# The up-projection of a diffusion block: weight sums and the gate product move from GpSimd to VectorE

## The chip, the cores and the metric

One core of a Trainium2 chip runs the whole block as one program. Five engines work beside each other, each through its own queue in order: TensorE (PE, with its weight loads as PEld) multiplies matrices, VectorE (DVE), ScalarE (ACT) and GpSimd (POOL) work element by element, and SyncE (SP) issues most of the DMAs. The metric is the device time of one execution in microseconds (us), lower is better.

## The reference, cut to what matters

The block is a norm, a token mixer (a state-space group and a differential attention group), an output projection, and a gated channel mixer. The change touches the channel mixer alone, and there the first matrix product:

```python
D_MODEL = 1024; SEQ = 1024; D_FF = 2816
def conv_ffn(h, w_up, cw, cb, w_down):
    val, gate = jnp.split(h @ w_up, 2, axis=-1)      # w_up: 1024 x 5632, float32
    gate = dwconv_centred(gate, cw, cb)              # width 3 over the 1024 tokens
    return (jax.nn.silu(gate) * val) @ w_down
```

Everything is float32. The kernel splits each float32 operand into a rounded high part and the low rest, and forms a product as high times high plus low times high plus high times low: three matmuls for one.

## The kernel before, in words

The hidden features lie on the 128 partitions, in 22 blocks of 128 for the value branch (0 to 21) and 22 for the gate branch (`NJ` = 22 onward). The tokens lie along the free dimension in two halves of 512. A `Unit` computes two neighbouring blocks of one branch over both halves with seven block products in place of eight (a Strassen-Winograd scheme). Its two weight tiles A0 and A1 (128 x 1024, 512 KB each, loaded by `raw_w`, four buffers named `wraw`) are each split into two halves of the contraction, so that a unit has four weight blocks, and combines them into sums `S` (`Unit.sums`, line 1205): S1 = A10 + A11, S2 = S1 - A00, S4 = A01 - S2 and S3 = A00 - A10. The matching sums of the activations (T1 to T4, B22) are made once, ahead of the loop.

The seven products of a unit come in the order P1, P2 (`p1`, `p2`, weights taken as they are), P3 (weight S4), P5 (S1), P6 (S2) in `p356`, and T3 (S3) and T4 (A11) in `rest`. Each is 12 matmuls of 128x128 by 128x512 into one of eight PSUM banks named `pu` (4 blocks of the contraction, three matmuls each). TensorE's order is pinned to the order of the code; the other engines' orders are chosen by a scheduler from its own estimate of times, so a change in one engine's load moves rows on others too.

Before a product can start, ScalarE rounds its weights (`whi`, line 125) and GpSimd or VectorE subtracts to get the low part (`wlo`, line 126). `whi` and `wlo` have three buffers each, so the rounding for a product waits until the product three places earlier is done. In the steady loop the low parts of P5 and T4 are VectorE's and the other five GpSimd's.

After the products, `rest` combines them: U2, U4, U3 (`add`, line 1226) and four outputs through `put`. For a gate unit `put_gate` adds into the tile `gt` (line 1251); `conv` then makes `u` by a scaled copy on ScalarE (line 1264), two multiply-adds on VectorE (lines 1265 and 1267) and a SiLU on ScalarE (line 1269). For a value unit `put_val` adds into a scratch tile `v` on VectorE (line 1257), and GpSimd multiplies `v` into `u` (line 1259). `gated` (line 1350) then makes four differences of the gated blocks on VectorE into a tile `T` and sends blocks and differences to memory (`gf_d`), from where the down-projection (`down`, tile names `pd`, `stg`) reads them back. `gt` and `T` share one buffer: the first `gt` of a pair waits until the `T` of the pair before has left.

The loop at the end of the function runs over j = 0, 2, ..., 20, one gate unit and one value unit each. For j = 0 (units `first`) and j = 2 (units `early`) some products are made ahead of the loop, while the activations' sums are still being formed.

Of the kernel before, what the change touches and what calls it, by code (L numbers as in the profile page):

```python
# [8 lines left out]
F32 = mybir.dt.float32  # L9
F32R = mybir.dt.float32r  # L10
AF = mybir.ActivationFunctionType
ALU = mybir.AluOpType
# [4 lines left out]
P = 128  # L17
# [86 lines left out]
class Prog:  # L104
# [934 lines left out]
    def mixffn(self, es, ssd_rest, e_pm):  # L1039
        nc, io = self.nc, self.io  # L1040
# [4 lines left out]
        op = self.pool(e_o, "mo", 2)  # L1045
# [50 lines left out]
        for dt in range(KT):  # L1096
            wa = self.load_w(io["wO"][dt][:, 8:12, :], kt=4)
            nc.sync.dma_start(x1[:, dt, :], io["xT"][:, dt, :])
            for t in range(2):
# [3 lines left out]
                                               in1=x1[:, dt, sls[t]], op0=ALU.mult, op1=ALU.add)  # L1103
# [86 lines left out]
        class Unit:  # L1190
# [11 lines left out]

            def sums(u, in0, in1, op):
                t = wp.tile([P, 4, P], F32, name="S", bufs=S_BUFS)
                nc.gpsimd.tensor_tensor(out=t, in0=in0, in1=in1, op=op)  # L1205
                return t

            def mul(u, src, T, eng=None):
# [30 lines left out]

            def rest(u, put):  # L1240
                U2 = u.add("U2", u.P6, u.X)
                put(0, 0, u.P2, u.X)
                U4 = u.add("U4", u.P5, U2)
                U3 = u.add("U3", u.mul(u.sums(u.sub(0, 0), u.sub(1, 0), ALU.subtract), T3), U2)
                put(0, 1, u.P3, U4)
                put(1, 1, u.P5, U3)
                put(1, 0, u.mul(u.sub(1, 1), T4, nc.vector), U3)

        def put_gate(gt):
            def put(i, t, ps, sb):  # L1250
                nc.vector.tensor_tensor(out=gt[:, i, sls[t]], in0=ps, in1=sb, op=ALU.add)
            return put

        def put_val(us):
            def put(i, t, ps, sb):
                v = vp.tile([P, 512], F32, name="v")
                nc.vector.tensor_tensor(out=v, in0=ps, in1=sb, op=ALU.add)
                o = us[i][:, sls[t]]
                nc.gpsimd.tensor_tensor(out=o, in0=o, in1=v, op=ALU.mult)
            return put  # L1260

        def conv(j, gate):
# [10 lines left out]
        first = Unit(NJ, 1), Unit(0, 1)  # L1273
# [47 lines left out]
        vp = self.pool(e_ffn, "vp", 2, side="right")  # L1321
        for j in range(0, NJ, 2):
# [5 lines left out]
            for u in (gate, val):  # L1328
                put = put_gate(gt) if u is gate else put_val(us)
# [305 lines left out]
```

## Time and profile before

| what | us |
|---|---|
| median of 3 runs | 1826.5 (1822.24 to 1832.29) |
| the profiled execution | 1826.04 |
| its span in the trace | 1824.2 |
| up-projection, starts of its first and last matmul | 1039.6 and 1535.2 |
| of this the pairs j = 4 to 20, nine alike | 1151.6 to 1535.4 |

The page of the profile gives for each engine its busy time and share of the span: TensorE 88%, VectorE 67%, GpSimd 59%, ScalarE 41%. Such shares are means over stages with different limits, so the stage itself is to be read. A busy TensorE is not TensorE at its peak, since a matmul's row also covers its pipeline; what counts is how far apart the matmuls start. The granted clock of TensorE is given as a share of full speed: 1.00 is 2.4 GHz, 0.50 is 1.2 GHz, and a stretch between the two had both.

### The profile page before, as it was taken

The numbers are of one execution on the slowest core, as the hardware profiler recorded it, in microseconds if no ns is written. First come the engines' busy times: TensorE is split into PE (matmuls) and PEld (weight loads), VectorE is DVE, ScalarE is ACT, GpSimd is POOL, SyncE is SP. The second block draws the span as 40 slices with busy tenths as digits, with TensorE's granted clock in tenths as the row PEclk, the third lists the DMA queues.
The fourth block names the chain that finished last, engine by engine and source line by source line (L and its number), as shares of the span: only waits on it lengthen the run. The fifth ranks groups of instructions, "written<-read, shape, count | busy, mean of one in ns | idle before, by whom it ended". The sixth has DMA issues, their size and how long they took to land.

```text
span 1824.2 us, 21276 instructions
## 1 busy us (share of the span) xinstructions
PE 1601.6 (88%) x7588; PEld 1266.8 (69%) x7588; DVE 1222.1 (67%) x1442; ACT 753.6 (41%) x1395; POOL 1081.2 (59%) x710
## 2 busy tenths in 40 slices
PE   6998998996999888888998958989989998989976
PEld 2797877784778655665677746767777776767755
DVE  4569633352656577877764588766667677898886
ACT  4533676631444333444443443333323334344242
POOL 3322678772100155658566767777778887778741
PEclk8999999998999899999999989999999998999997
DMA  8276767667131667447553312222222225744222
GB/s 310 96 241 218 239 217 246 242 215 224 56 104 46 197 218 213 127 143 234 179 166 114 107 47 98 87 87 93 98 87 87 100 99 187 252 156 127 67 75 93
DMA packets 138826, 273.35 MB, mean 150 GB/s; under 512 B 11984, under 2 KB 60544, under 8 KB 138208
## 3 DMA queue, kind: packets, MB, share of 16 engines
q1 hardware_dynamic: 138128, 271.03, 45.0%
q8 instruction: 60, 0.98, 0.2%
q0 software_dynamic: 592, 0.96, 0.2%
q14 instruction: 46, 0.38, 0.1%
HBM read 197.63 MB, written 74.32 MB: 149 GB/s over the span
## 4 chain that ended last, share of the span: by engine, by line
PE 39%; DVE 18%; POOL 17%; DMA 11%; issue 8%; ACT 6%; SPq 0%; POOLq 0%; DVEq 0%; ACTq 0%
PE pu L145 9%; POOL wlo L126 6%; PE pd L145 6%; POOL S L1205 4%; PE lat L145 4%; PE pz L145 3%; PE pb L145 3%; PE sc L145 3%; DMA K<-kd 3%; PE pw L145 2%; DVE T L126 2%; DMA wt<-wmB 2%; DMA gd<-R 2%; PE po L145 2%; DMA R<-atd 2%
## 5 line engine op out<-in xcount | busy, mean ns | idle before, releaser
L145 PE MATMUL pu<-T,whi 128*128 128x512 f32 x1232 | 387.8, 396 | 8.7 <-ACT whi L125 8.7
L145 PE MATMUL pu<-T,wlo 128*128 128x512 f32 x616 | 248.7, 404 | 44.5 <-POOL wlo L126 36.9
L145 PEld LDWEIGHTS pu<-T,whi 128*128 128x128 f32 x1232 | 235.8, 191 | 58.2 <-ACT whi L125 9.1
L126 POOL TENSOR_TENSOR wlo<-wraw,whi 128x512 fp32r<-128x512 f32 (+2 forms) x118 | 163.4, 1388 | 101.3 <-ACT whi L125 101.2
L145 PE MATMUL lat<-hl,w_hi 128*128 128x512 f32 x640 | 204.6, 396 | 3.0 <-DVE tm L685 2.1
L145 PE MATMUL pd<-T,whi 128*128 128x512 f32 x560 | 183.2, 408 | 15.1 <-ACT whi L125 7.5
L126 POOL TENSOR_TENSOR w_lo<-w_raw,w_hi 128x1024 fp32r<-128x1024 f32 (+1 forms) x36 | 82.7, 2299 | 178.7 <-ACT w_hi L125 156.9
L126 POOL TENSOR_TENSOR wlo<-S,whi 128x512 fp32r<-128x512 f32 (+2 forms) x122 | 171.0, 1411 | 27.6 <-ACT whi L125 27.6
L145 PEld LDWEIGHTS pu<-T,wlo 128*128 128x128 f32 x616 | 117.8, 191 | 86.2 <-POOL wlo L126 49.3
L814 DVE TENSOR_REDUCE stat<-sc 128x1 f32<-128x1280 f32 x64 | 95.2, 1488 | 104.2 <-PE sc L145 104.2
L125 ACT CAST whi<-wraw 128x512 fp32r<-128x512 f32 (+2 forms) x140 | 81.3, 583 | 196.8 <-PE pu L145 108.8
L125 ACT CAST whi<-S 128x512 fp32r<-128x512 f32 (+2 forms) x144 | 81.9, 573 | 150.0 <-PE pu L145 94.7
L145 PEld LDWEIGHTS lat<-hl,w_hi 128*128 128x128 f32 x640 | 121.8, 191 | 28.5 <-DVE tm L685 2.5
L145 PEld LDWEIGHTS pd<-T,whi 128*128 128x128 f32 x560 | 109.5, 197 | 44.2 <-DVE T L126 12.3
L815 ACT ACTIVATE et<-sc,stat 128x1280 f32<-128x1280 f32 x64 | 85.1, 1330 | 130.0 <-DVE stat L814 128.4
L145 PE MATMUL sc<-K,S 128*128 128x512 f32 (+1 forms) x384 | 97.5, 390 | 45.8 <-DMA K<-kd 24.1
L145 PE MATMUL pd<-T,wlo 128*128 128x512 f32 x280 | 115.3, 412 | 15.5 <-POOL wlo L126 15.3
L145 PE MATMUL lat<-hl,w_lo 128*128 128x512 f32 x320 | 126.8, 396 | 0.0
L145 PEld LDWEIGHTS sc<-K,S 128*128 128x128 f32 x384 | 73.5, 200 | 72.8 <-ACT et L815 30.1
L538 POOL TENSOR_TENSOR R<-R,never 128x1024 f32<-128x1024 f32 x32 | 80.6, 2533 | 43.1 <-DMA R<-atd 41.4
L542 ACT ACTIVATE R<-R,lna 128x128 f32<-128x128 f32 x256 | 78.3, 393 | 56.7 <-POOL R L538 56.6
L908 POOL TENSOR_TENSOR xw<-xt,dte 128x1024 f32<-128x1024 f32 x18 | 36.8, 2049 | 93.7 <-DMA xt<-xtok 71.4
(280 smaller groups left out, 3682.0 us busy)
## 6 DMA issues: line engine op xcount, KB each, us to landing
wraw<-wUp SPq DMA_DIRECT2D x46, 512.0 KB, 3.3
wt<-wmB SPq DMA_DIRECT2D x32, 512.0 KB, 4.5
R<-atd SPq DMA_DIRECT2D x32, 512.0 KB, 5.6
stg<-gf_d SPq DMA_DIRECT2D x21, 768.0 KB, 4.8
w_raw<-wU SPq DMA_DIRECT2D x28, 512.0 KB, 5.1
gf_d<-T SPq DMA_DIRECT2D x11, 1024.0 KB, 4.2
K<-kd SPq DMA_DIRECT2D x32, 320.0 KB, 7.8
xt<-xtok SPq DMA_DIRECT2D x19, 512.0 KB, 5.2
```

The costliest lines, as they stand in the source:

```text
L125: nc.scalar.copy(hi, src)
L126: (lo_eng or nc.vector).tensor_tensor(out=lo, in0=src, in1=hi, op=ALU.subtract)
L145: self.pe(self.nc.tensor.matmul(out, lhsT=lhsT, rhs=rhs, start=start, stop=stop))
L538: nc.gpsimd.tensor_tensor(out=R[:, d], in0=R[:, d], in1=self.never[:, d].unsqueeze(1).broadcast_to([P, 8, P]), op=ALU.add)
L542: nc.scalar.activation(e, e, AF.Exp, bias=self.lna[:, d, i, h:h + 1], scale=1.0)
L814: nc.vector.tensor_reduce(out=st[:, c:c + 1], in_=sc, axis=AX.X, op=ALU.max, negate=True)
L815: nc.scalar.activation(et, sc, AF.Exp, bias=st[:, c:c + 1], accum_out=acc)
L908: nc.gpsimd.tensor_tensor(out=h3(xw), in0=h3(xt), in1=bc_h(self.dte, d, i), op=ALU.mult)
L1205: nc.gpsimd.tensor_tensor(out=t, in0=in0, in1=in1, op=op)
```

## The change

Three edits in the up-projection:

- the sums S of all units but the two of j = 0 are made on VectorE (80 of 88);
- the value branch is added in place, into the PSUM bank that holds the product, and VectorE multiplies it into `u` from there; the scratch tile `v` goes, except for one output of the early value unit, which is kept in SBUF from before the loop and goes the old way (43 of 44 products move);
- with that, GpSimd keeps the low parts of the weights and little else.

```diff
             def sums(u, in0, in1, op):
                 t = wp.tile([P, 4, P], F32, name="S", bufs=S_BUFS)
-                nc.gpsimd.tensor_tensor(out=t, in0=in0, in1=in1, op=op)
+                (nc.gpsimd if u in first else nc.vector).tensor_tensor(out=t, in0=in0, in1=in1, op=op)
                 return t
...
-                put(0, 0, u.P2, u.X)
+                put(0, 0, u.P2, u.X, u.early)
...
-            def put(i, t, ps, sb):
+            def put(i, t, ps, sb, sbuf=False):
                 nc.vector.tensor_tensor(out=gt[:, i, sls[t]], in0=ps, in1=sb, op=ALU.add)
...
-            def put(i, t, ps, sb):
-                v = vp.tile([P, 512], F32, name="v")
+            def put(i, t, ps, sb, sbuf=False):
+                v = vp.tile([P, 512], F32, name="v") if sbuf else ps
                 nc.vector.tensor_tensor(out=v, in0=ps, in1=sb, op=ALU.add)
                 o = us[i][:, sls[t]]
-                nc.gpsimd.tensor_tensor(out=o, in0=o, in1=v, op=ALU.mult)
+                (nc.vector if v is ps else nc.gpsimd).tensor_tensor(out=o, in0=v, in1=o, op=ALU.mult)
```

The scheduler then orders the queues anew. GpSimd's queue before, over a value unit of the loop: the first rows are sums of the gate unit still to come, mixed with the low parts of the running unit.

```order
L1205 TENSOR_TENSOR S_10186<-wraw_10143 128x512 [waits DMAHW3_49]
L1205 TENSOR_TENSOR S_10188<-S_10186,wraw_10141 128x512 [waits DMAHW7_49,Pool_49]
L126 TENSOR_TENSOR wlo_10006<-wraw_9831,whi_10005 128x512 [waits Activation_49]
L126 TENSOR_TENSOR wlo_10029<-S_10025,whi_10028 128x512 [waits DVE_49,Activation_49]
L1205 TENSOR_TENSOR S_10190<-wraw_10141,S_10188 128x512 [waits Pool_49]
L1205 TENSOR_TENSOR S_10248<-wraw_10141,wraw_10143 128x512 [waits DVE_49]
L1259 TENSOR_TENSOR u_9975<-u_9975,v_10080 128x512 [waits DMAHW5_49,DVE_49]
L126 TENSOR_TENSOR wlo_10063<-S_10023,whi_10062 128x512 [waits Activation_49]
L126 TENSOR_TENSOR wlo_10089<-S_10085,whi_10088 128x512 [waits Activation_49]
L126 TENSOR_TENSOR wlo_10152<-wraw_10141,whi_10151 128x512 [waits Activation_49]
```

After, the same place holds the low parts alone.

```order
L126 TENSOR_TENSOR wlo_9991<-wraw_9816,whi_9990 128x512 [waits Activation_49]
L126 TENSOR_TENSOR wlo_10014<-S_10010,whi_10013 128x512 [waits DVE_49,Activation_49]
L126 TENSOR_TENSOR wlo_10048<-S_10008,whi_10047 128x512 [waits Activation_49]
L126 TENSOR_TENSOR wlo_10073<-S_10069,whi_10072 128x512 [waits Activation_49]
L126 TENSOR_TENSOR wlo_10133<-wraw_10122,whi_10132 128x512 [waits DMAHW7_49,Activation_49]
L126 TENSOR_TENSOR wlo_10152<-wraw_10122,whi_10151 128x512 [waits Activation_49]
```

The sums and the multiplication are gone from between them: what is in front of a low part on GpSimd is now only another low part.

VectorE's queue before, at the end of a value unit and the start of the next gate unit: the last output, the differences T, the low part of P5 and the first `gt`, which waits for the DMA of T and so holds what follows it.

```order
L1257 TENSOR_TENSOR v_10129<-pu_10112,U3_10104 128x512 [waits PE_49]
L1350 TENSOR_TENSOR T_10132<-u_9980,T_10132 128x512 [waits DVE_49,Pool_49]
L1350 TENSOR_TENSOR T_10132<-u_9980,u_9975 128x512
L126 TENSOR_TENSOR wlo_10211<-S_10186,whi_10210 128x512 [waits PE_49,Activation_49]
L1350 TENSOR_TENSOR T_10132<-u_9980,T_10132 128x512 [waits DVE_49,Pool_49]
L1251 TENSOR_TENSOR gt_10149<-pu_10169,X_10167 128x512 [waits DMAHW2_49,DVE_49,PE_49]
L126 TENSOR_TENSOR wlo_10273<-wraw_10143,whi_10272 128x512 [waits DMAHW3_49,Activation_49]
```

After, at the same place.

```order
L1257 TENSOR_TENSOR pu_10094<-pu_10094,U3_10088 128x512 [waits PE_49]
L1259 TENSOR_TENSOR u_9965<-pu_10029,u_9965 128x512 [waits DVE_49]
L1259 TENSOR_TENSOR u_9965<-pu_10094,u_9965 128x512 [waits DVE_49]
L1350 TENSOR_TENSOR T_10113<-u_9965,T_10113 128x512 [waits DVE_49]
L1350 TENSOR_TENSOR T_10113<-u_9965,u_9960 128x512
L1205 TENSOR_TENSOR S_10320<-wraw_10126,S_10318 128x512 [waits Pool_49]
L1350 TENSOR_TENSOR T_10113<-u_9965,T_10113 128x512 [waits DVE_49]
L126 TENSOR_TENSOR wlo_10192<-S_10167,whi_10191 128x512 [waits PE_49,Activation_49]
L1205 TENSOR_TENSOR S_10379<-wraw_10126,wraw_10128 128x512 [waits DVE_49]
L1251 TENSOR_TENSOR gt_10130<-pu_10150,X_10148 128x512 [waits DMAHW2_49,PE_49]
L126 TENSOR_TENSOR wlo_10254<-wraw_10124,whi_10253 128x512 [waits Activation_49]
```

The multiplications stand between the last output and the differences, and two sums (S4 and S3 of the next value unit) around the low part of P5; the order of T, low part and `gt` is as it was.

VectorE's queue before, from the second `gt` of a gate unit to the low part of P5 of the value unit behind it.

```order
L1251 TENSOR_TENSOR gt_10149<-pu_10192,U4_10246 128x512 [waits DVE_49]
L1226 TENSOR_TENSOR U3_10267<-pu_10250,U2_10243 128x512 [waits PE_49]
L1251 TENSOR_TENSOR gt_10149<-pu_10209,U3_10267 128x512 [waits DVE_49]
L1265 SCALAR_TENSOR_TENSOR u_10289<-gt_10149,c_fcw_89,u_10289 128x1023 [waits DMAHW5_49,Activation_49]
L1251 TENSOR_TENSOR gt_10149<-pu_10271,U3_10267 128x512 [waits PE_49]
L1267 SCALAR_TENSOR_TENSOR u_10289<-gt_10149,c_fcw_89,u_10289 128x1023 [waits DVE_49]
L1265 SCALAR_TENSOR_TENSOR u_10294<-gt_10149,c_fcw_89,u_10294 128x1023 [waits DMAHW1_49,DMAHW0_49,Activation_49]
L1267 SCALAR_TENSOR_TENSOR u_10294<-gt_10149,c_fcw_89,u_10294 128x1023 [waits DVE_49]
L126 TENSOR_TENSOR wlo_10360<-S_10335,whi_10359 128x512 [waits PE_49,Activation_49]
```

After, at the same place, with the sum that now stands ahead of it.

```order
L1205 TENSOR_TENSOR S_10477<-wraw_10434 128x512 [waits DMAHW3_49,Pool_49]
L1251 TENSOR_TENSOR gt_10130<-pu_10173,U4_10227 128x512 [waits DVE_49]
L1205 TENSOR_TENSOR S_10479<-S_10477,wraw_10432 128x512 [waits DMAHW7_49,DVE_49,Pool_49]
L1226 TENSOR_TENSOR U3_10248<-pu_10231,U2_10224 128x512 [waits PE_49]
L1251 TENSOR_TENSOR gt_10130<-pu_10190,U3_10248 128x512 [waits DVE_49]
L1265 SCALAR_TENSOR_TENSOR u_10270<-gt_10130,c_fcw_89,u_10270 128x1023 [waits DMAHW5_49,Activation_49]
L1251 TENSOR_TENSOR gt_10130<-pu_10252,U3_10248 128x512 [waits PE_49]
L1267 SCALAR_TENSOR_TENSOR u_10270<-gt_10130,c_fcw_89,u_10270 128x1023 [waits DVE_49]
L1205 TENSOR_TENSOR S_10481<-wraw_10432,S_10479 128x512 [waits Pool_49]
L1265 SCALAR_TENSOR_TENSOR u_10275<-gt_10130,c_fcw_89,u_10275 128x1023 [waits DMAHW1_49,DMAHW0_49,Activation_49]
L1267 SCALAR_TENSOR_TENSOR u_10275<-gt_10130,c_fcw_89,u_10275 128x1023 [waits DVE_49]
L126 TENSOR_TENSOR wlo_10341<-S_10316,whi_10340 128x512 [waits PE_49,Activation_49]
```

Three sums have come in ahead of that low part. The first of them waits for a weight load (`DMAHW3`).

## Rows read from the trace of the kernel before

**Rows 1.** Chain that ended last: shares of the span by engine and by line

```profile
PE 39%; DVE 18%; POOL 17%; DMA 11%; issue 8%; ACT 6%; SPq 0%; POOLq 0%; DVEq 0%; ACTq 0%
PE pu L145 9%; POOL wlo L126 6%; PE pd L145 6%; POOL S L1205 4%; PE lat L145 4%; PE pz L145 3%; PE pb L145 3%; PE sc L145 3%; DMA K<-kd 3%; PE pw L145 2%; DVE T L126 2%; DMA wt<-wmB 2%; DMA gd<-R 2%; PE po L145 2%; DMA R<-atd 2%
```

**Rows 2.** By stretch: length, busy PE, PEld, DVE, ACT, POOL (instructions), granted clock, DMA, GB/s

```profile
1114.20:1151.56 37.36, 29.25 (x121) 21.98 (x120) 32.02 (x28) 13.03 (x18) 29.08 (x17) 1.00 0.28 98
1151.56:1535.43 383.87, 359.32 (x1513) 286.08 (x1511) 255.56 (x235) 127.42 (x184) 300.41 (x201) 0.98 0.29 100
1535.43:1565.00 29.57, 21.95 (x71) 14.43 (x71) 29.52 (x32) 15.11 (x30) 18.47 (x15) 0.83 0.80 282
```

**Rows 3.** The same view: three products without a wait, one product with

```profile
1256.65:1264.81 8.16, 8.16 (x37) 6.76 (x36) 7.72 (x9) 4.20 (x5) 5.41 (x4) 1.00 0.20 64
1219.48:1228.57 9.09, 4.60 (x14) 3.32 (x12) 7.55 (x4) 4.24 (x5) 8.93 (x6) 0.81 0.17 58
```

**Rows 4.** Waits over the nine pairs: us in total, times, longest us

```profile
DVE gt L1251 <- DMA gf_d<-T: 41.7, 9, 5.6
...
PE pu L145 <- POOL wlo L126: 21.3, 15, 4.5
...
POOL S L1205 <- DMA wraw<-wUp: 19.3, 14, 4.0
...
PE pu L145 <- DVE wlo L126: 3.2, 8, 0.6
```

**Rows 5.** Timeline of TensorE in the long wait: start us, us, instruction [idle before]

```profile
1224.35 0.50 PE L145 MATMUL pu<-T,wlo 128*128 128x512 f32 x1 [4.49 <-POOL wlo L126]
```

**Rows 6.** Groups of GpSimd, nine pairs: busy us, mean ns | idle before

```profile
L126 POOL TENSOR_TENSOR wlo<-S,whi 128x512 fp32r<-128x512 f32 x54 | 78.1, 1458 | 0.8 <-ACT whi L125 0.8
L126 POOL TENSOR_TENSOR wlo<-wraw,whi 128x512 fp32r<-128x512 f32 x35 | 58.0, 1657 | 45.0 <-ACT whi L125 45.0
L1259 POOL TENSOR_TENSOR u<-u,v 128x512 f32<-128x512 f32 x37 | 51.8, 1399 | 0.9 <-DVE v L1257 0.8
```

**Rows 7.** Groups of VectorE, nine pairs, same columns

```profile
L1265 DVE SCALAR_TENSOR_TENSOR u<-gt,c_fcw,u 128x1023 f32<-128x1023 f32 x18 | 37.2, 2066 | 0.0
L1267 DVE SCALAR_TENSOR_TENSOR u<-gt,c_fcw,u 128x1023 f32<-128x1023 f32 x18 | 34.9, 1936 | 0.3
L1350 DVE TENSOR_TENSOR T<-u 128x512 f32<-128x512 f32 x18 | 31.8, 1769 | 6.8 <-POOL u L1259 6.8
L126 DVE TENSOR_TENSOR wlo<-S,whi 128x512 fp32r<-128x512 f32 x18 | 30.6, 1700 | 0.0
L1226 DVE TENSOR_TENSOR U<-pu,U 128x512 f32<-128x512 f32 x36 | 24.9, 691 | 8.2 <-PE pu L145 7.6
L1350 DVE TENSOR_TENSOR T<-u,T 128x512 f32<-128x512 f32 x18 | 22.0, 1220 | 16.5 <-POOL u L1259 16.5
L126 DVE TENSOR_TENSOR wlo<-wraw,whi 128x512 fp32r<-128x512 f32 x18 | 19.9, 1106 | 34.8 <-ACT whi L125 34.8
```

**Rows 8.** Line 1265, whole run: ns least/median/most, first and last start

```profile
L1265 DVE SCALAR_TENSOR_TENSOR u<-gt,c_fcw,u x22: 1274/2114/2317, 1106.5 to 1517.8; 128x1023 f32<-128x1023 f32 x22
```

**Rows 9.** Timeline of VectorE ahead of the loop, GpSimd waiting

```profile
1082.53 3.09 DVE L126 TENSOR_TENSOR T<-x,T 128x512 fp32r<-128x512 f32 x5
```

**Rows 10.** Timeline of GpSimd at that time

```profile
1078.44 9.51 POOL L126 TENSOR_TENSOR wlo<-S,whi 128x512 fp32r<-128x512 f32 x1 [4.81 <-ACT whi L125]
```

**Rows 11.** DMA issues: KB each, median us from issue to landing

```profile
wraw<-wUp SPq DMA_DIRECT2D x46, 512.0 KB, 3.3
...
gf_d<-T SPq DMA_DIRECT2D x11, 1024.0 KB, 4.2
```

**Rows 12.** Timeline of TensorE at the start of the down-projection

```profile
1544.61 1.22 PE L145 MATMUL pd<-T,whi 128*128 128x512 f32 x2 [2.83 <-DVE T L126]
```

**Rows 13.** Timeline of VectorE ahead of that wait's end

```profile
1541.68 1.48 DVE L1350 TENSOR_TENSOR T<-u 128x512 f32<-128x512 f32 x1
1543.08 2.08 DVE L126 TENSOR_TENSOR T<-stg,T 128x512 fp32r<-128x512 f32 x2
```

## Prediction

> **What bounds the kernel now.** I read the chain of waits first: TensorE holds 39% of it, but GpSimd 17%, and by line the low parts (line 126) and sums (line 1205) of GpSimd are its second and fourth entry [rows 1]. So the next question is what GpSimd costs in the up-projection, and there the table by stretch is the view: in the nine pairs alike GpSimd is busy 300.41 of 383.87 us and VectorE 255.56 [rows 2]. Then the price without waits. Three products that wait for nothing take 8.16 us at a granted clock of 1.00, 2.4 GHz [rows 3], so one takes 2.72 us, a pair of 14 takes 38.1 us, and nine pairs 342.7. The nine pairs lose 383.9 - 342.7 = 41.2 us, 4.6 each. The pair j = 2 has 10 products in its stretch, 27.2 us at that price, and takes 37.36 [rows 2]: 10.2 lost.
>
> Whose loss it is stands in the waits: TensorE waits 21.3 us for GpSimd's low parts and 3.2 us for VectorE's [rows 4]. The rest of the 41.2 comes behind the long ones: in the worst, a product of 9.09 us in place of 2.72, TensorE stood 4.49 us for a low part of GpSimd [rows 5] and the granted clock of the whole product was 0.81 [rows 3], so a part of it ran at 1.2 GHz. GpSimd is late because its queue is in order: ahead of a low part stand sums and multiplications, and the sums themselves wait 19.3 us for weight loads [rows 4].
>
> **The change part by part.** *GpSimd.* The nine pairs keep the 54 + 35 low parts, 136.1 us as measured [rows 6], of 300.4; the sums and the 37 multiplications (51.8 us) go. A low part now starts as soon as its rounding is done. The rounding for a product can start when the product three places earlier ends, two products or 5.4 us ahead of its own start; an instruction of ScalarE takes 127.42 / 184 = 0.69 us there in the mean [rows 2] and a low part 1.46 even with VectorE in its way [rows 6]. That leaves 5.4 - 0.7 - 1.5, about 3 us of cover for each low part. So I set GpSimd's 21.3 us of waits, and what the clock loses behind them, to nothing; what could use the cover up is the third rival.
>
> *VectorE, the added work.* A pair gets 8 sums and 4 multiplications. A difference of two SBUF tiles with nothing in its way takes 0.62 us (five in 3.09 [rows 9]). The multiplication takes one operand from PSUM, as line 1226 does in 0.69 us [rows 7]. That is 8 x 0.62 + 4 x 0.69 = 7.7 us. No large row of VectorE writes PSUM, as the in-place add now does. I take 0.69 for it too, by the nearest row; the bounds are 0.62, as if it cost nothing beyond SBUF, and twice 0.69, if reading and writing one bank took turns, which is 4 x 0.69 = 2.8 us more a pair.
>
> *VectorE, the blocked time.* Rows of VectorE with one operand in PSUM take 0.69 us each time, those with two in SBUF 1.1 to 1.8 where 0.62 would do, and the multiply-adds about 2.0 where 1.27 has been seen [rows 7, 8]. The six groups of that kind hold 176.4 us; clear, they would hold 36 x 1.27 + 72 x 0.62 = 90.4. So VectorE is blocked for 86.0 us, 9.6 a pair, while GpSimd runs 201 operations in the nine pairs, 22.3 each [rows 2]: 0.43 us an operation. With 10 low parts a pair in place of 22.3 that is 4.3 us. But each of them now meets 20 VectorE operations that can be blocked where it met 12. I take 5 us. The bounds: none, if VectorE's stream keeps GpSimd out as it did ahead of the loop, where one low part took 9.51 us [rows 10] beside a stream of VectorE [rows 9]; and 10 x 1.15 = 11.5, if each blocks one VectorE operation as long as in the worst group (1.77 - 0.62 [rows 7]).
>
> The Trainium skill (SBUF — State Buffer, Who interferes with whom) has it that a VectorE instruction with two SBUF inputs and a GpSimd instruction that reads SBUF exclude each other, and that the one that comes second is held for the whole of the first. The groups agree in which forms grow and which don't. What it says against this change: eight sums a pair move to the side where each can be held, and only the four multiplications, with one input in PSUM, are free of it. The sum by its hardest reading stands behind the fourth rival.
>
> *VectorE's loop.* VectorE's own work of a pair is then (255.6 - 86.0) / 9 = 18.8, plus 7.7, plus 5 blocked: 31.5 us. That is below 38.1, but three transfers lie in its loop. `gt` shares a buffer with T, so the first `gt` waits for T's DMA, 4.2 us [rows 11], while only a low part and a sum run, 1.2 us: 3.0 idle. And twice a pair the first sum stands behind the low part of T4, whose end starts the weight load that this sum reads: 3.3 us [rows 11], with two PSUM adds in between, 1.4: 1.9 idle, 3.8 a pair. The loop is 31.5 + 3.0 + 3.8 = 38.3, as long as TensorE's 38.1. Before, the waits for weight loads were GpSimd's; now they hold all that is behind them on VectorE: `gt`, the multiply-adds and the low part of P5. With two loops of equal length that wait for each other, I add 1.2 us a pair, mostly as waits of TensorE for the low part of P5: 39.3.
>
> *The sum.* Nine pairs: 9 x 39.3 = 353.7, 30.2 less than now; bounds 38.1 (342.7, 41.2 less) and 11.5 blocked with it (44.8 us a pair, 403.2, 19.3 more); the in-place adds at their upper bound alone make the loop 41.1 and the forecast some 16 to 25 later. Pair j = 2: the waits for GpSimd go, but VectorE is already busy 32.02 of 37.36 us there [rows 2] and gets sums and multiplications too; half of the 10.2 goes, 5 less (9 less to 3 more). Ahead of the loop one added PSUM row comes in front of the activations' sums: 0.7 more. Start of the down-projection: it stands 2.83 us [rows 12], and more before, for VectorE's splits, which are mixed with differences T that wait for GpSimd's multiplications [rows 13]; with the multiplications on VectorE these waits go: 3 less (6 less, or 3 more since VectorE is the busy engine there, 29.52 of 29.57 [rows 2]). Together -30.2 - 5 + 0.7 - 3 = -37.5, from the profiled execution's 1826.0, which is 0.5 below the median: 1788.5, so I say 1789. The down-projection behind 1565 and all before 1050 keep their order.
>
> **The rivals.** *First, better: TensorE's floor.* VectorE is blocked under 4 us a pair and its loop hides below TensorE's. The nine pairs take 342.7, pair 2 and the start of the down-projection lose little: -41.2 - 9 - 5 + 0.7 gives 1771. For it speaks the row of 9.51 us, where VectorE wasn't held at all [rows 10]; against it, that two loops of one length rarely run without a gap.
>
> *Second, no change: VectorE takes GpSimd's place.* VectorE is held as long as now, 9.6 us a pair, since it has 20 operations that can be held in place of 12. The loop is 26.5 + 9.6 + 6.8 = 42.9, 386.1 in all, 2 more than now; with half of the other gains it ends at 1820 to 1828. For it: the 0.43 us an operation may grow with the number of VectorE operations it can meet, 0.43 x 20/12 x 10 = 7.2, most of the way. Against it: GpSimd's 136.1 us are 38% of the 353.7, so many of these meet nobody.
>
> *Third: GpSimd kept out.* Between the second multiply-add and the low part of P5, VectorE now has three multiply-adds, a sum and a low part in a row, 3 x 1.27 + 2 x 0.62 = 5.1 us with no PSUM operation between, and a stream like that kept GpSimd out for 9.51 us [rows 10]. A low part that misses the gap ahead of it has 3 us of cover and costs 2 us a pair, 18 us in all: 1807. It speaks against it that the gap, a `gt` from PSUM, comes just when that low part is ready.
>
> *Fourth, slower: each low part holds VectorE in full.* Ten holds of 1.15 us make 11.5, the loop 44.8 us, and the nine pairs take 403.2, 19.3 more; VectorE in that state gives nothing in pair 2 or at the down-projection: 1846. It decides from the point where blocked time passes 42.65 - 33.3 = 9.4 us a pair (42.65 is a pair now), or where the in-place adds cost 2.8 more and 6.6 is enough. Against it: GpSimd's operations come one at a time now, with gaps.
>
> The rule of the Trainium skill (SBUF — State Buffer, Who interferes with whom) in its hardest reading, ten holds of a whole low part of 1.46 us [rows 6], gives an estimate of 14.6 us a pair, a loop of 47.9 and 1874 in all; the trace shows no group held by more than 1.15 in the mean.
>
> **How the numbers follow.** My forecast 0.50, the floor 0.22, GpSimd kept out 0.07, no change 0.13, slower 0.08. A measurement can tell 0.5%, 9 us, from no change. Faster by more than that (below 1817): 0.50 + 0.22 + 0.07, less 0.02 of the forecast's upper end, 0.77. Within: 0.15. Slower: 0.08. The likeliest case by itself runs from 1779 to 1803. The range that holds 8 in 10 takes most of the floor and reaches to no change: 1773 to 1822.
>
> **What would show it.** Right: TensorE's waits for GpSimd's low parts nearly gone, no product with a clock below 1.00 in the nine pairs, a pair of 38.5 to 40 us; GpSimd busy some 130 to 140 us there; waits left mostly for VectorE's `wlo`; a sum on VectorE that waits for `wraw`. VectorE's multiplications and in-place adds at 0.69 us. Wrong: two-input groups of VectorE still at 1.7 us (blocked time above 9 us a pair), in-place adds well over 0.69, or low parts of GpSimd above 3 us. The forecast fails altogether if VectorE's loop is longer than 42.65 us a pair.

## The result, and the profile after

The changed kernel takes 1785.2 us (median of 4 runs, 1783.77 to 1786.59) against 1827.84 (4 runs) for the kernel before beside it: a ratio of 0.977, 95% interval 0.9745 to 0.9794. The forecast was 1789, so the time is where it was put. The experiments show that the reason given for it was only a part of the truth.

The chain of waits of the changed kernel, shares of the span by engine and by line, answers to [rows 1].

```profile
PE 22%; DVE 6%; POOL 3%; issue 2%; DMA 2%; ACT 0%; DVEq 0%; POOLq 0%; ACTq 0%
```

GpSimd's share was 17% before and is 3% now, but the two can't be set against each other: this chain is followed over a third of the span only (its shares add up to 35%, those of before to 99%). The table by stretch is the safer view. Here it is, with the columns of [rows 2], for pair j = 2, the nine pairs and the start of the down-projection.

```profile
1114.06:1145.14 31.08, 29.21 (x121) 23.51 (x120) 29.11 (x36) 13.85 (x18) 13.17 (x8) 0.95 0.32 111
1145.14:1492.65 347.51, 344.57 (x1513) 282.94 (x1511) 258.86 (x344) 128.05 (x184) 136.49 (x97) 1.00 0.33 112
1492.65:1522.25 29.60, 21.58 (x76) 15.69 (x76) 24.74 (x35) 15.34 (x31) 16.62 (x11) 0.88 0.85 304
```

The nine pairs take 36.4 us less and stand 347.5 - 342.7 = 4.8 us above TensorE's price without waits, at a granted clock of 1.00 throughout. Pair j = 2 takes 6.3 less, the start of the down-projection the same as before. Together that is 42.6, and the span is 42.2 shorter.

Waits of the changed kernel over the nine pairs, to be read against [rows 4].

```profile
DVE gt L1251 <- DMA gf_d<-T: 29.5, 9, 4.4
...
DVE S L1205 <- DMA wraw<-wUp: 7.0, 7, 2.0
PEld pu L145 <- DVE wlo L126: 5.9, 9, 2.2
...
PE pu L145 <- DVE wlo L126: 2.8, 2, 1.8
```

TensorE waits for no low part of GpSimd any more. The sums, now VectorE's, wait 7.0 us for weight loads where GpSimd's had waited 19.3.

Groups of VectorE there (busy us, mean ns, then idle before), with those of [rows 7].

```profile
L1205 DVE TENSOR_TENSOR S<-wraw 128x512 f32<-128x512 f32 x34 | 28.9, 849 | 12.6 <-DMA wraw<-wUp 7.0 <-POOL wlo L126 5.4
L1267 DVE SCALAR_TENSOR_TENSOR u<-gt,c_fcw,u 128x1023 f32<-128x1023 f32 x18 | 27.6, 1532 | 0.3
L1226 DVE TENSOR_TENSOR U<-pu,U 128x512 f32<-128x512 f32 x38 | 26.0, 686 | 1.2 <-PE pu L145 0.6
L1265 DVE SCALAR_TENSOR_TENSOR u<-gt,c_fcw,u 128x1023 f32<-128x1023 f32 x18 | 25.4, 1411 | 0.0
L1259 DVE TENSOR_TENSOR u<-pu,u 128x512 f32<-128x512 f32 x37 | 24.4, 678 | 0.1
L126 DVE TENSOR_TENSOR wlo<-S,whi 128x512 fp32r<-128x512 f32 x18 | 20.0, 1109 | 0.0
L1257 DVE TENSOR_TENSOR pu<-pu,U 128x512 f32<-128x512 f32 x29 | 19.8, 688 | 0.0
...
L1350 DVE TENSOR_TENSOR T<-u 128x512 f32<-128x512 f32 x19 | 13.7, 720 | 0.0
```

The forms with two inputs in SBUF have shrunk: T from 1769 to 720 ns, the multiply-adds from about 2000 to 1411 and 1532. The multiplication from PSUM (line 1259) and the add in place in PSUM (line 1257) take 678 and 688 ns.

### The profile page after: what moved, and what is told of

It is laid out like the page before. It is cut to its first block, busy times and chain, and to the rows that moved or that the text cites. A ratio compares the mean times of both kernels' runs of the same rounds, so it can differ in the third digit from the quotient of the medians.

```text
span 1782.0 us, 21245 instructions
## 1 busy us (share of the span) xinstructions
PE 1587.1 (89%) x7588; PEld 1266.6 (71%) x7588; DVE 1224.6 (69%) x1565; ACT 752.7 (42%) x1395; POOL 887.5 (50%) x587
## 5 line engine op out<-in xcount | busy, mean ns | idle before, releaser
L145 PE MATMUL pu<-T,wlo 128*128 128x512 f32 x616 | 243.1, 395 | 16.1 <-POOL wlo L126 11.3
L126 POOL TENSOR_TENSOR wlo<-wraw,whi 128x512 fp32r<-128x512 f32 (+2 forms) x118 | 156.4, 1328 | 148.9 <-ACT whi L125 147.2
L145 PE MATMUL sc<-K,S 128*128 128x512 f32 (+1 forms) x384 | 97.3, 389 | 46.6 <-DMA K<-kd 24.8
L145 PEld LDWEIGHTS sc<-K,S 128*128 128x128 f32 x384 | 73.5, 200 | 73.5 <-ACT et L815 30.2
L145 PE MATMUL pz<-hl,w_hi 128*128 128x512 f32 x256 | 90.0, 408 | 0.0
```

The costliest lines, as they stand in the source:

```text
L126: (lo_eng or nc.vector).tensor_tensor(out=lo, in0=src, in1=hi, op=ALU.subtract)
L145: self.pe(self.nc.tensor.matmul(out, lhsT=lhsT, rhs=rhs, start=start, stop=stop))
```

## The experiments

The length of the nine pairs (first matmul of j = 4 to the end of the last) is the sharpest measure: the stage ahead, which no edit touches, started the up-projection anywhere from 1033.4 to 1044.0 us in the profiled executions. Each length is that of one execution; kernels that share the loop agree closely (347.51 for the changed kernel and 347.88 for e7; 342.72, 342.93 and 342.74 for e4, e8 and e10). The lengths, with the busy time of VectorE and GpSimd from the table by stretch:

| kernel | sums | multiplication | nine pairs | VectorE | GpSimd |
|---|---|---|---|---|---|
| before | GpSimd | GpSimd | 383.87 | 255.56 | 300.41 |
| changed | VectorE | VectorE | 347.51 | 258.86 | 136.49 |
| e1 | VectorE | GpSimd | 388.99 | 280.36 | 193.03 |
| e2 | GpSimd | VectorE | 347.02 | 246.09 | 240.95 |
| e5: e1, gt and T apart | VectorE | GpSimd | 349.69 | 267.54 | 194.16 |
| e6: before, gt and T apart | GpSimd | GpSimd | 364.20 | 259.73 | 296.05 |
| e9: e2, GpSimd filled | GpSimd | VectorE | 355.35 | 257.74 | 285.67 |
| e3: changed, sums twice | VectorE | VectorE | 383.86 | 336.71 | 144.45 |
| e4: changed, low parts on VectorE | VectorE | VectorE | 342.72 | 293.50 | 11.91 |

### e1: the sums alone

```diff
-                v = vp.tile([P, 512], F32, name="v") if sbuf else ps
+                v = vp.tile([P, 512], F32, name="v")
...
-                (nc.vector if v is ps else nc.gpsimd).tensor_tensor(out=o, in0=v, in1=o, op=ALU.mult)
+                nc.gpsimd.tensor_tensor(out=o, in0=o, in1=v, op=ALU.mult)
```

> Only the sums move to VectorE; the multiplications stay on GpSimd with the scratch tile v. Theory Q (the queue): the 41.2 us of the nine pairs were low parts standing behind sums in GpSimd's queue, and the sums' waits for weight loads (19.3 us) with them. Without the sums GpSimd has 10 low parts and 4 multiplications a pair, 20 of 38 us; one or two multiplications of 1.4 us ahead of a low part stay inside its 3 us of cover. Nine pairs 348 to 356, in all 1786 to 1797. Rival C (contention): the gain came from operations that no longer exclude each other, and a third of the removed GpSimd operations is back: two thirds of the gain, 28 us, so 1798 to 1804, and the multiply-adds and T differences of VectorE stay above 1.6 us.

Measured 1829.55, ratio 1.003 (1.0004 to 1.0055): no gain at all, and both theories missed. Waits over the nine pairs:

```profile
DVE gt L1251 <- DMA gf_d<-T: 37.5, 9, 5.3
...
PEld pu L145 <- DVE wlo L126: 27.2, 19, 4.2
PE pu L145 <- DVE wlo L126: 20.4, 10, 3.8
...
DVE S L1205 <- DMA wraw<-wUp: 19.2, 15, 2.3
```

GpSimd's queue was relieved, as theory Q wanted, and TensorE's waits for it went. But the same wait for weight loads, 19.2 us for 19.3 [rows 4], now stands on VectorE, and TensorE waits for VectorE's low part of P5 behind it. Moving the sums moved the wait with them, so the loads come late for another reason.

### e2: the multiplication alone

```diff
-                (nc.gpsimd if u in first else nc.vector).tensor_tensor(out=t, in0=in0, in1=in1, op=op)
+                nc.gpsimd.tensor_tensor(out=t, in0=in0, in1=in1, op=op)
```

> Only the multiplications move to VectorE, from PSUM; all sums stay on GpSimd. Theory Q: the sums with their waits for loads still stand ahead of the low parts, so TensorE still waits for GpSimd's low parts for 10 us or more in the nine pairs; a third of the gain at the most, 1812 to 1822. Rival C: GpSimd's operations fall from 22.3 to 18.2 a pair and blocked time with them by a fifth, 1817 to 1826. Rival M (the multiplications were what held the low parts up, since they wait for VectorE and for the SiLU): most of the gain is here, 1785 to 1800.

Measured 1781.21, ratio 0.9771 (0.9745 to 0.9798): rival M, and a little below its numbers: all of the gain, with the eight sums a pair still in GpSimd's queue. Three groups of VectorE in the nine pairs:

```profile
L1265 DVE SCALAR_TENSOR_TENSOR u<-gt,c_fcw,u 128x1023 f32<-128x1023 f32 x18 | 36.6, 2035 | 0.0
L1267 DVE SCALAR_TENSOR_TENSOR u<-gt,c_fcw,u 128x1023 f32<-128x1023 f32 x18 | 34.3, 1904 | 0.3
...
L126 DVE TENSOR_TENSOR wlo<-S,whi 128x512 fp32r<-128x512 f32 x18 | 13.3, 740 | 0.0
```

The multiply-adds are held as long as before [rows 7], and the nine pairs still are at 347.0, far from rival C's numbers. But VectorE is held less in all: the low part of P5 fell from 1700 to 740 ns, and by the prediction's reckoning (1.27 us for a multiply-add, 0.62 for the others) 52 us of the nine pairs are blocked, where it was 86. So e2 alone does not rule out that contention cost a part of the time; e5 and e6 bear on it.

### What the multiplication holds up

The worst wait of TensorE before the change [rows 5], followed back beyond GpSimd's queue, shows it. VectorE of the kernel before (start us, us, instruction, idle before):

```profile
1205.54 0.68 DVE L1350 TENSOR_TENSOR T<-u,T 128x512 f32<-128x512 f32 x1
1211.72 0.69 DVE L1251 TENSOR_TENSOR gt<-pu,X 128x512 f32<-128x512 f32 x1 [5.50 <-DMA gf_d<-T]
1212.33 1.74 DVE L126 TENSOR_TENSOR wlo<-wraw,whi 128x512 fp32r<-128x512 f32 x1
```

SyncE's queue of the same kernel:

```profile
1206.25 0.37 SPq L1354 DMA_DIRECT2D gf_d<-T  x1
1214.11 0.33 SPq L1122 DMA_DIRECT2D wraw<-wUp  x1
```

And its GpSimd:

```profile
1217.50 2.38 POOL L1205 TENSOR_TENSOR S<-wraw 128x512 f32<-128x512 f32 x1 [3.97 <-DMA wraw<-wUp]
1219.96 2.13 POOL L1205 TENSOR_TENSOR S<-S,wraw 128x512 f32<-128x512 f32 x1
1222.05 2.25 POOL L126 TENSOR_TENSOR wlo<-wraw,whi 128x512 fp32r<-128x512 f32 x1
```

The last T ends at 1206.2, its DMA is issued at 1206.25, the first gt starts when that has left (1211.72), the low part of T4 stands behind gt and ends at 1214.07, which frees a weight tile, so the load is issued at 1214.11; the sum waits for it until 1217.50, the low part of P2 behind the sums ends at 1224.30, and TensorE goes on at 1224.35. Each step starts where the last one ends. The same `gt` makes the rounding of P2 late by a second path, over ScalarE:

```profile
1216.16 1.25 ACT L1264 ACTIVATE u<-gt,c_fcb,c_fcw 128x1024 f32<-128x1024 f32 x1 [4.00 <-DVE gt L1251]
1217.32 0.60 ACT L125 CAST whi<-wraw 128x512 fp32r<-128x512 f32 x1
```

So the low part of P2 could have started at 1217.92, but stood behind the two sums until 1222.05. At the head of all this stands T, and T waits for GpSimd's multiplications (6.8 and 16.5 us of idle time in [rows 7]). From the end of a value unit's last product to the end of the last T are 9.5 us before and 9.1 in e1, but 5.8 in the changed kernel and 5.7 in e2; to the first gt 14.2 and 14.1 against 10.3 and 10.3 (means over eight turns, from the starts and durations in the traces).

### e5 and e6: the chain cut

A buffer each for gt and T; e5 has it on e1, e6 on the kernel before. To make room, U2 has one buffer and U3 and U4 share one, for which the add that makes U3 moves behind the output that reads U4; what these side edits cost was not timed by itself.

```diff
-        T = gp.tile([P, 4, 512], F32, tag="gt", name="T")
+        T = gp.tile([P, 4, 512], F32, tag="gt", name="T", bufs=2)
...
-            gt = gp.tile([P, 2, SEQ], F32, tag="gt", name="gt")
+            gt = gp.tile([P, 2, SEQ], F32, tag="gt", name="gt", bufs=2)
```

> The kernel with only the sums on VectorE (nine pairs 389.0 us, multiplications on GpSimd), with a buffer each for gt and T, so that the first gt of a pair no longer waits for the DMA of T; for the room, U2 and U3/U4 have one buffer each. Theory K (chain): what the multiplication on GpSimd costs is the lateness of T (9.1 us after the value unit's last product, against 5.7 with the multiplication on VectorE), which runs on over the DMA of T, the first gt (14.1 against 10.3) and the low part of T4 behind it to the weight load, the sums, the multiply-adds and the low part of P5. With a buffer each, the first gt starts with its product, the chain is cut, and the multiplications on GpSimd cost little: nine pairs 345 to 360, in all 1780 to 1800. Rival G (GpSimd's time, 193 us, or its contention): the multiplications still hold VectorE up, whatever gt waits for: 375 to 389, 1815 to 1830.

Measured 1783.74, ratio 0.9786 (0.974 to 0.9831), nine pairs 39.3 us shorter than in e1. Theory K holds. Waits there:

```profile
PEld pu L145 <- DVE wlo L126: 7.1, 12, 2.9
...
DVE S L1205 <- DMA wraw<-wUp: 6.0, 12, 0.6
```

Against e1's, the wait of gt is gone and the sums wait 6.0 us in place of 19.2, though GpSimd multiplies as before and T is as late (9.1 us). VectorE's blocked time fell by 12 us only, from 76 to 64, so contention is not what the 39.3 us were.

> The kernel before with the same buffer edit and nothing else: sums and multiplications stay on GpSimd, 300 us of work there in the nine pairs. Theory K: T as late as before, but gt and the low part of T4 do not wait for it, the weight loads come earlier and GpSimd's sums do not wait for them: nine pairs 345 to 362, in all 1785 to 1803. Rival Q (GpSimd's queue is too full for the low parts whatever the loads do): 370 to 384, 1810 to 1826.

Measured 1806.71, ratio 0.99 (0.9874 to 0.9926): between the two. The cut alone brings 383.87 - 364.20 = 19.7 us, with VectorE blocked as long as before (90 us by the same reckoning, for 86). Waits there:

```profile
PEld pu L145 <- POOL wlo L126: 17.6, 22, 1.3
...
PE pu L145 <- POOL wlo L126: 8.0, 12, 0.9
```

The waits for GpSimd left are many and short, none above 1.3 us where 4.5 stood [rows 4]. They look like the full queue that the prediction named, 296.05 us of work in 364.20; e9 tests that.

### e9: GpSimd filled again

```diff
+                if v is ps:
+                    d = vp.tile([P, 512], F32, name="v")
+                    nc.gpsimd.tensor_tensor(out=d, in0=o, in1=o, op=ALU.mult)
```

> The kernel with only the multiplications on VectorE (nine pairs 347.0), and for each of them GpSimd makes a product of the same size into a scratch tile that nobody reads. GpSimd is as full as before (300 us) and its rows stand where the multiplications stood, but T does not wait for them. Two parts of the loss are to be told apart: the chain through T (19.7 us: 383.9 to 364.2 when it was cut with GpSimd still full) and GpSimd's full queue (the other 21.5). Theory both: the chain stays short, the queue is full again: nine pairs 358 to 368, in all 1793 to 1808. Rival chain alone (a full queue costs nothing while T is early): 347 to 353, 1780 to 1788. Rival queue alone: 378 to 389, 1815 to 1828.

Measured 1792.44, ratio 0.9832 (0.9803 to 0.9861), nine pairs 355.35: just under what "both" wanted and above "chain alone". With T early, a GpSimd with 285.67 us of work costs 355.35 - 347.02 = 8.3 us. The added product was rated at 51.8 us [rows 6] and took 48.7. It also holds VectorE, busy 257.74 us for e2's 246.09, so the 8.3 are the full queue and the contention that comes with it, which no run separates. So of the 36.9 us between the kernel before and e2, 19.7 go when the chain is cut and 8.3 come back when GpSimd is filled. The other 8.9 are in neither; that they are the two together, a late load in front of a full queue, is likely but not shown.

### e3: VectorE's turning point

```diff
-                (nc.gpsimd if u in first else nc.vector).tensor_tensor(out=t, in0=in0, in1=in1, op=op)
+                for _ in range(1 if u in first else 2):
+                    (nc.gpsimd if u in first else nc.vector).tensor_tensor(out=t, in0=in0, in1=in1, op=op)
```

> The changed kernel with each VectorE sum made twice into the same tile: 8 more operations of 0.62 us a pair, with the blocked time seen in the sums (0.79 in the mean) 6.3 us. Theory S (slack): VectorE's loop in the changed kernel is 28.8 busy + 3.3 for the DMA of T + 0.8 for weight loads = 32.9 us a pair against TensorE's 38.6, so 5.7 us of the 6.3 are hidden: 0 to 15 us more, 1785 to 1800. Rival L (loops of one length, as the forecast's own sum had it, with 3.8 us a pair for the two weight loads): all of it shows, 9 x 6.3 = 57 more, 1835 to 1845.

Measured 1814.02, ratio 0.9951 (0.993 to 0.9972): some 33 us above the changed kernel (0.9951 against 0.977 of 1823.72), below L and above S. The table by stretch:

```profile
1143.48:1527.34 383.86, 355.09 (x1513) 286.69 (x1511) 336.71 (x421) 130.07 (x188) 144.45 (x97) 0.98 0.29 102
```

VectorE got (336.71 - 258.86) / 9 = 8.7 us a pair, not the 6.3 expected: a sum of the first kind took 1007 ns in the mean where it takes 849 in the changed kernel, probably because the doubled sums meet more of GpSimd's rows; a pair grew by (383.86 - 347.51) / 9 = 4.0. So 4.6 us a pair were hidden: the changed kernel has slack on VectorE, not far below the 5.7 of theory S, and the loops are not of one length.

### e4: all low parts on VectorE

```diff
-                product(ps, parts(src, eng), T, True, True)
+                product(ps, parts(src, eng or nc.vector), T, True, True)
```

> The changed kernel with the low parts of all units but the two of j = 0 on VectorE too, so that GpSimd does next to nothing in the nine pairs. No operation of VectorE can be held there: multiply-adds 1.27, differences 0.62 to 0.69. Theory S: VectorE's loop is 28.8 - 3.6 blocked + 10 x 0.62 + 3.3 + 0.8 = 35.5 us a pair, under 38.6, but five more low parts a unit stand in its queue behind multiply-adds and the wait of gt for the DMA of T: nine pairs 347 to 365, in all 1785 to 1803, and TensorE's waits are for VectorE's low parts. Rival L (3.8 us for the weight loads): a loop of 38.5 and more waits, 1800 to 1815. Rival C: contention was what cost the time, so without any the nine pairs reach the floor of 342.7, 1778 to 1782.

The edit reaches further than its expectation says: of the units of j = 0 only the low parts of P3 and P5 stay on GpSimd, so the start changes too.

Measured 1773.58, ratio 0.9741 (0.9696 to 0.9785), an interval that overlaps the changed kernel's (0.9745 to 0.9794): the total does not tell the two apart, the stretches do. The table by stretch, and two groups of VectorE:

```profile
1133.05:1475.77 342.72, 342.72 (x1513) 283.54 (x1511) 293.50 (x435) 130.41 (x187) 11.91 (x9) 1.00 0.32 114
```

```profile
L126 DVE TENSOR_TENSOR wlo<-S,whi 128x512 fp32r<-128x512 f32 x72 | 49.5, 689 | 5.7 <-ACT whi L125 5.7
...
L1267 DVE SCALAR_TENSOR_TENSOR u<-gt,c_fcw,u 128x1023 f32<-128x1023 f32 x20 | 26.2, 1309 | 0.0
```

TensorE is at its floor, 342.72, without a wait, and e8 and e10 repeat it. With GpSimd all but idle no row of VectorE is held: a low part takes 0.69 us where GpSimd took 1.43, a multiply-add of line 1267 takes 1.31. VectorE took 91 more rows for 34.6 us more busy time, 0.38 us each. The floor came as rival C's number had it, but contention is not the main part of the 41.2 us lost before: in e2 the multiply-adds were held as before, 52 us of VectorE were blocked, and TensorE lost only 4.3 us. The Trainium skill (SBUF — State Buffer, Who interferes with whom) says that a VectorE instruction with two SBUF inputs and a GpSimd read exclude each other; the rows of e4, clear once GpSimd is silent, agree.

### e7, e8 and e10: the two ends

At the start of the down-projection the changed kernel shows waits of TensorE:

```profile
1497.66 1.22 PE L145 MATMUL pd<-T,whi 128*128 128x512 f32 x2 [4.14 <-DVE T L126]
...
1508.14 0.80 PE L145 MATMUL pd<-T,wlo 128*128 128x512 f32 x1 [2.79 <-POOL wlo L126]
```

VectorE and GpSimd ahead of the second:

```profile
1501.14 6.10 DVE L126 TENSOR_TENSOR T<-stg,T 128x512 fp32r<-128x512 f32 x10
```

```profile
1502.12 6.93 POOL L126 TENSOR_TENSOR wlo<-S,whi 128x384 fp32r<-128x384 f32 x2 [5.06 <-ACT whi L125]
```

A stream of ten VectorE rows without a gap kept GpSimd out, as in [rows 9, 10] at the start. Waits of TensorE over the start of the down-projection, first of the kernel before, then of the changed one:

```profile
PE pd L145 <- DVE T L126: 7.5, 8, 2.8
```

```profile
PE pd L145 <- DVE T L126: 5.2, 4, 4.1
PE pd L145 <- POOL wlo L126: 2.8, 1, 2.8
```

e7 gives VectorE the low parts of the first unit of the down-projection and, at the other end, those of P3 and P5 of the two units of j = 0: the letters of `E_W` stand for P3, P5 and P6, so the edit takes in P5 beside the P3 that the expectation names.

```diff
-E_W = "ggv"
+E_W = "vvv"
...
-                product(ps, parts(w, eng[e]), T[name], True, True)
+                product(ps, parts(w, eng["v" if blk.k0 == 0 and u == 0 else e]), T[name], True, True)
```

> The changed kernel with the low parts of the first products of both ends on VectorE: P3 of the two units of j = 0, and the first unit of the down-projection. Theory X (VectorE's stream keeps GpSimd out there): at the start the product with a wait of 10 us loses 2 to 4 in its place, 6 to 9 us gained; at the down-projection the wait of 2.8 us for GpSimd goes with the half clock behind it, 3 to 5 gained; in all 1768 to 1775. Rival Y (the low parts were late because their S or their rounding was late, not because GpSimd was kept out): both waits stay, now for VectorE, 1778 to 1785.

Measured 1780.85, ratio 0.9762 (0.9722 to 0.9801), not to be told from the changed kernel by its time, and within rival Y's numbers. By place, theory X holds at the down-projection: from its first to its last matmul it fell from 274.4 to 269.7 us. One execution is not much for that (e3, without the edit, took 270.4), but the first 72 matmuls took 24.1 to 24.8 us in the three kernels with the edit (e7, e8, e10) and 27.4 to 30.2 in the nine without. The start did not gain. The changed kernel, by stretch: the two products P3 of j = 0, then all up to pair j = 2.

```profile
1066.98:1092.17 25.19, 8.01 (x25) 5.78 (x24) 19.93 (x26) 8.68 (x16) 19.67 (x8) 0.65 0.06 21
1092.17:1114.06 21.89, 21.89 (x98) 17.94 (x96) 17.94 (x25) 7.44 (x11) 4.01 (x3) 1.00 0.30 97
```

The same two stretches of e7:

```profile
1071.11:1092.22 21.11, 10.22 (x26) 7.32 (x24) 21.11 (x29) 9.07 (x17) 10.07 (x5) 0.67 0.07 25
1092.22:1117.98 25.76, 22.76 (x98) 17.78 (x97) 18.68 (x26) 6.94 (x10) 5.33 (x4) 1.00 0.24 82
```

47.1 and 46.9 us: the 4.1 gained are lost in the next stretch. VectorE, busy through the whole of the first stretch in e7, kept GpSimd out once more, now from one of the sums of j = 0 that the change leaves there, and VectorE's own next sum then waited for a weight load. GpSimd, SyncE's queue and VectorE of e7:

```profile
1087.59 5.90 POOL L1205 TENSOR_TENSOR S<-wraw 128x512 f32<-128x512 f32 x1 [8.45 <-DVE wlo L126]
```

```profile
1093.51 0.33 SPq L1122 DMA_DIRECT2D wraw<-wUp  x1
```

```profile
1096.95 0.69 DVE L1205 TENSOR_TENSOR S<-wraw 128x512 f32<-128x512 f32 x1 [4.62 <-DMA wraw<-wUp]
```

The sum on GpSimd took 5.90 us (1.28 in the changed kernel), its end at 1093.49 frees the weight tile for the load issued at 1093.51 (1091.75 in the changed kernel), and VectorE stands idle until that has landed. TensorE waits 3.0 us in all for the low parts behind it. So moving the low parts moved the wait to a sum; whether moving that sum too would gain was not tried.

> All low parts of the up-projection on VectorE and those of the first unit of the down-projection. The nine pairs stay at the floor of 342.7 as with the low parts of the loop on VectorE alone (1773.6); the start has one wait less for GpSimd (1 to 4 us) and the down-projection one (3 to 5): 1764 to 1770 by theory X, 1772 to 1776 by rival Y.

e8 puts e4 and e7 together: 1764.82, ratio 0.9677 (0.9633 to 0.9722), within theory X's numbers and faster than the kernel before and the changed one; nine pairs 342.93.

> The low parts of the loop and of the first unit of the down-projection on VectorE; those of P3 of j = 0 are GpSimd's again, since moving them only moved the wait at the start (the start took 72.5 us with them on GpSimd and 75.0 without). By that 2.5 us less than the 1764.8 measured, 1760 to 1766. If the difference at the start was no more than the spread of single executions, 1763 to 1768.

e10, which leaves P3 and P5 of j = 0 on GpSimd, took 1771.16, ratio 0.9702 (0.9676 to 0.9727): above both expectations. The intervals of e8 and e10 overlap, and e10's profiled execution began the up-projection 6.4 us later than e8's (1042.99 against 1036.56), so the totals do not say which of the two starts is better. By place e10's is: from the first matmul to pair j = 2 it took 72.5 us, as in e4, and e8 took 75.0.

## Why the prediction was right, and where it was not

**Where the time was lost.** Right: 41.2 us in the nine pairs, and 36.4 of them went; TensorE's waits for GpSimd's low parts are gone and the clock is 1.00.

**Why GpSimd was late.** This is the step that fell short, in the prediction's words: "GpSimd is late because its queue is in order: ahead of a low part stand sums and multiplications". The last link is as it says: in the worst wait a low part that was ready at 1217.92 stood behind two sums until 1222.05. But it takes the queue's content for the cause, and by that the sums, with their waits of 19.3 us, should bring a large share when they go. e1 and e2 show the opposite: the sums alone bring nothing, the multiplications alone everything. A full GpSimd is worth 8.3 us by itself (e9); the larger part was the chain that starts with T (e5, e6). The prediction saw three of its pieces, as idle time of VectorE: T behind the multiplications, gt behind T's DMA, the sum behind the load. It priced them singly and did not join them.

**The added work.** Right: multiplications 0.68, adds in place 0.69 us. The doubled price of the upper bound did not come.

**The blocked time.** Forecast 5 us a pair. By the same reckoning as before (1.27 for a multiply-add, 0.62 for the others) the groups of two SBUF inputs, the 68 sums with them, hold 165.6 us where 133.1 would do: 32.5, 3.6 a pair. About a third of that is overlap of rows, not holding: e4's rows read 0.69 and 1.28 to 1.31 with GpSimd silent, and by these the groups are held for some 22 us, 2.4 a pair.

**VectorE's loop.** Forecast 38.3, as long as TensorE's. Measured 258.86 / 9 = 28.8 of work, 3.3 for gt and 0.8 for weight loads: 32.9. Two terms are mis-sized: the weight loads, 3.8 against 0.8, and the work, 31.5 against 28.8, of which 1.4 is blocked time. In e1 the loads cost 2.1 a pair (19.2 / 9), in e5, where T is as late but the weight tile does not wait for it, 0.7 (6.0 / 9): how long a sum waits hangs on when the low part of T4 frees the tile, and the prediction took the load's duration for every pair. e3 bears the slack out. So the first rival, TensorE's floor, was nearer in this stretch: a pair loses 0.5 us, not the 1.2 forecast.

**Pair j = 2 and the start.** 6.3 us less for a forecast of 5; the loop's start at 1114.06 against 1114.20, where 0.7 more was expected.

**The down-projection.** Forecast 3 less, measured none (29.60 against 29.57). TensorE's waits for VectorE's splits did fall, by 7.5 - 5.2 = 2.3 us, but the third rival's mechanism took their place here, where no one had looked for it: 2.8 us of wait, and a granted clock of 0.52 over the 3.1 us behind it, 1.2 GHz for nearly all of them, because VectorE's splits now come as an unbroken stream. e7 gets 4.1 back there (28.9 to 24.8 us for the first 72 matmuls).

**The sum.** -42.3 in the profiled executions (1826.04 to 1783.77) for -37.5. That it came so near is in part luck: the change moved the sums and the multiplications together, and the mechanism did not say which of them mattered. The same words for the sums alone are theory Q of e1, 1786 to 1797, and that took 1829.55.

## What to carry to other kernels

Follow a wait back past the queue that ends it, over buffers, stores and loads, until a step is reached that started on time: the instruction to move is the one at the head of that chain, or the buffer in its middle is the one to double; here four multiplications a pair were worth all that eight sums were not. When an edit has two parts, time each alone; a sum that comes out right does not show which term earned it. A helper engine that holds up the engine it helps can cost more than it saves: taking the last ten low parts a pair from GpSimd brought TensorE to its floor.

## What the runs showed of the hardware

Reading and writing one PSUM bank in the same VectorE instruction cost no more than reading it (688 ns in place, 686 ns into SBUF at line 1226 after the change). Beside ten VectorE rows without a gap (6.10 us) two GpSimd rows of 128x384 took 6.93 us at the down-projection; at the start before the change a single one of 128x512 took 9.51 [rows 10], and in e7 a sum took 5.90. Where both engines run with gaps, each loses: in the changed kernel's nine pairs a low part of 128x512 takes GpSimd 1.43 us in the mean, with rows of 1.28 among them, and VectorE's low part of P5 takes 1.11, against 0.69 with GpSimd silent.
